# Sixty-four zero bytes per partition, written to the output early, in a kernel that combines two expert outputs

## The chip, the cores and the metric

The kernel runs on one core of a Trainium2 chip. Its time is the device time in microseconds (us) of that core, as a median over several runs. The profile shows one execution of the same program; its span, from the first to the last recorded event, is a little shorter than the time measured.

## The reference: what is computed

For each of 16 x 1024 tokens there are two expert outputs of 512 floats and two weights. The result is their weighted sum.

```python
batch, seq, hidden, n_experts, k = 16, 1024, 512, 8, 2
expert_outputs   # (batch, seq, k, hidden), float32: 67.1 MB
combine_weights  # (batch, seq, k), float32: 0.13 MB

weights = combine_weights[..., np.newaxis]
return np.sum(expert_outputs * weights, axis=2)   # (batch, seq, hidden): 33.6 MB
```

All in all 100.8 MB cross between HBM and SBUF, with three floating-point operations for each element of the result.

## The kernel before

The 16384 tokens are laid over the 128 partitions: 120 tokens a partition in the main part and 8 in a last part. The main part goes through SBUF in ten tiles of 12 tokens a partition (6 MB each), and the last part is an eleventh tile of 4 MB. Four tile buffers rotate, so the fifth load can only start when the first tile's store has read its buffer out. The result of a tile is written over the front half of its buffer and stored from there.

```python
    J, LAST = 12, 8
    main = per - LAST                       # per = 128 tokens a partition
    ...
    def rows(x):
        a = x[0 : P * main, :].rearrange("(p t) f -> p t f", p=P)
        b = x[P * main : n, :].rearrange("(p t) f -> p t f", p=P)
        return lambda t, c: a[:, t : t + c, :] if t < main else b[:, t - main : t - main + c, :]

    eo, cw, o = rows(eo), rows(cw), rows(o)
    ...
    ipool = ctx.enter_context(tc.tile_pool(name="in", bufs=4))

    wt = wpool.tile([P, per * k], dt)

    for t, c in ((0, main), (main, LAST)):  # two weight loads, 120 KB and 8 KB
        nc.scalar.dma_start(
            out=wt[:, k * t : k * (t + c)].rearrange("p (t k) -> p t k", k=k), in_=cw(t, c)
        )

    warm = wpool.tile([P, 1], dt)
    nc.scalar.activation(out=warm, in_=nc.const_aps.tensor(1.0, (P, 1), dt), func=copy)

    for g in range(last + 1):
        et = ipool.tile([P, J, k * h], dt)
        ot = et.rearrange("p j f -> p (j f)")[:, 0 : J * h].rearrange("p (j f) -> p j f", f=h)
        t0, c = g * J, J if g < last else LAST

        # the first tile comes in two pieces: 2 tokens, then 10
        for a, m in ((0, 2), (2, c - 2)) if g == 0 else ((0, c),):
            nc.sync.dma_start(
                out=et[:, a : a + m],
                in_=eo(t0 + a, m),
                max_dma_last_dim=k * h * 4 if g + a == 0 else None,
            )
        if g < last - 1:                    # nine tiles: two VectorE operations and a store
            ...
            nc.vector.tensor_tensor(out=ek, in0=ek, in1=wb, op=mult)                            # L78
            nc.vector.tensor_tensor(out=ot, in0=et[:, :, 0:h], in1=et[:, :, h : 2 * h], op=add) # L79
            nc.scalar.dma_start(out=o(t0, c), in_=ot)                                           # L80
            continue
        ...                                 # the last two tiles share the work with ScalarE
        nc.sync.dma_start(out=o(t0, c), in_=ot[:, 0:c])
```

Loads are issued from SyncE's queue (q1 in the profile). The weights and the stores of the first nine tiles are issued from ScalarE's queue (q10), and the stores of the last two tiles from SyncE's.

The very first load piece is cut into packets of 4096 B (`max_dma_last_dim`); a packet of the other loads is a whole row of 40960 or 49152 B, and of a full tile's store 24576 B.

Of the kernel before, what the change touches and what calls it, by code (L numbers as in the profile page):

```python
# [1 line left out]

# [4 lines left out]


@with_exitstack
def kernel(  # L10
    ctx: ExitStack,
    tc: tile.TileContext,
    expert_outputs: bass.AP,
    combine_weights: bass.AP,
    out: bass.AP,
):

    nc = tc.nc  # L20
    b, s, k, h = expert_outputs.shape
    assert k == 2
    n = b * s
    P = nc.NUM_PARTITIONS
    per = n // P
    assert per * P == n
    J, LAST = 12, 8
    main = per - LAST
    assert main % J == 0
    eo = expert_outputs.rearrange("b s k h -> (b s) (k h)")  # L30
    cw = combine_weights.rearrange("b s k -> (b s) k")
    o = out.rearrange("b s h -> (b s) h")
# [9 lines that stand above are left out]
    dt = mybir.dt.float32  # L42
    mult = mybir.AluOpType.mult
    add = mybir.AluOpType.add
    copy = mybir.ActivationFunctionType.Copy

    last = main // J

    wpool = ctx.enter_context(tc.tile_pool(name="w", bufs=1))
    ipool = ctx.enter_context(tc.tile_pool(name="in", bufs=4))  # L50

    wt = wpool.tile([P, per * k], dt)

    for t, c in ((0, main), (main, LAST)):
        nc.scalar.dma_start(
# [18 lines that stand above are left out]
        if g < last - 1:  # L74

            wb = wt[:, g * J * k : (g + 1) * J * k].unsqueeze(2).to_broadcast([P, J * k, h])
            ek = et.rearrange("p j (k h) -> p (j k) h", k=k)
# [6 lines that stand above are left out]
        for i in range(c):  # L84
            t = t0 + i
            nc.scalar.activation(  # L86
                out=et[:, i, 0:h], in_=et[:, i, 0:h], func=copy, scale=wt[:, 2 * t : 2 * t + 1]
            )
            if g == last:
                nc.vector.scalar_tensor_tensor(  # L90
                    out=ot[:, i, :],
                    in0=et[:, i, h : 2 * h],
                    scalar=wt[:, 2 * t + 1 : 2 * t + 2],
                    in1=et[:, i, 0:h],
                    op0=mult,
                    op1=add,
                )
        if g < last:
            w1 = wt.rearrange("p (t k) -> p t k", k=k)[:, t0 : t0 + c, 1:2]
            x1 = et[:, :, h : 2 * h]  # L100
            nc.vector.tensor_tensor(out=x1, in0=x1, in1=w1.to_broadcast([P, c, h]), op=mult)  # L101
            nc.vector.tensor_tensor(out=ot, in0=et[:, :, 0:h], in1=x1, op=add)  # L102
        nc.sync.dma_start(out=o(t0, c), in_=ot[:, 0:c])


# [1 line left out]
_INS = ['expert_outputs', 'combine_weights']  # L107
_OUTS = [((16, 1024, 512), 'float32')]


# [23 lines left out]
```

## Time and profile before

| what | value |
|---|---|
| time, median of 3 runs | 239.03 us (238.98 to 239.05) |
| span of the profiled execution | 237.3 us |
| VectorE (DVE): L78, 9 times | 116.6 us, 12955 ns each |
| VectorE: L79, 9 times | 59.0 us, 6558 ns each |
| ScalarE (ACT): L86, 20 times | 12.5 us, 707 ns each |
| a tile load of 6 MB, issue to landing | 29.9 us (median of 9) |
| a tile store of 3 MB, issue to landing | 32.7 us (median of 9 from ScalarE's queue) |
| weights, 120 KB and 8 KB, issue to landing | 4.4 and 17.1 us |

In the profile's lists an instruction is named by its source line (L78 is line 78 of the kernel before), its engine, and what it writes and reads. A busy share is the part of the span in which an engine worked. "Issue to landing" runs from the instruction that starts a transfer to the arrival of its last byte, so it holds the time in which the transfer stood in line behind others. The chain of waits is followed back from the last instruction, at each step to what released it.

### The profile page before, as it was taken

To read this page: it belongs to the slowest core of one execution; us is meant where nothing else is said; L and a number is where in the kernel's file an instruction comes from. 1 tells how busy PE (TensorE), PEld (TensorE's weight loads), DVE (VectorE), ACT (ScalarE), POOL (GpSimd) and SP (SyncE) were. 2 spreads that over 40 slices of the span, in tenths; PEclk is the share of its full clock that TensorE was granted. 3 is DMA by queue.
4 is the path that set the end of the run, shared out by engine and by line. 5 is a ranking of instruction groups with operands and counts; after the bars stand their busy time and mean duration, and the time that the engine had idled before them with its cause. 6 is when DMAs were issued, how large, how long until landed. Compare 5 with 4: busy or idle time off the path is not lost.

```text
span 237.3 us, 154 instructions
## 1 busy us (share of the span) xinstructions
DVE 193.9 (82%) x28; ACT 14.0 (6%) x22; POOL 0.2 (0%) x4
## 2 busy tenths in 40 slices
DVE  0008999999999999999999879969996998785710
ACT  2000000000000000000000000000000000740800
POOL 0000000000000000000000000000000000000000
DMA  8999999989899999999897999999997979999997
GB/s 308 443 456 406 398 431 497 398 356 505 356 439 435 427 464 464 398 398 522 348 522 344 452 427 435 464 464 398 398 522 340 530 336 460 458 403 442 402 438 309
DMA packets 3728, 100.80 MB, mean 425 GB/s; under 512 B 528, under 2 KB 656, under 8 KB 912
## 3 DMA queue, kind: packets, MB, share of 16 engines
q1 hardware_dynamic: 2144, 72.35, 71.1%
q10 hardware_dynamic: 1584, 28.44, 27.9%
HBM read 67.24 MB, written 33.55 MB: 425 GB/s over the span
## 4 chain that ended last, share of the span: by engine, by line
DMA 59%; DVE 33%; ACT 2%; DVEq 0%; ACTq 0%; issue 0%; SPq 0%
DMA et<-in_expert_outputs_dram 30%; DMA out_dram<-et 29%; DVE et L78 22%; DVE et L79 11%; ACT et L86 2%; DVE et L90 1%; DVEq L129 0%; ACTq L129 0%; SPq L69 0%; DVEq L78 0%; ACTq L86 0%
## 5 line engine op out<-in xcount | busy, mean ns | idle before, releaser
L78 DVE TENSOR_TENSOR et<-et,wt 128x12288 f32<-128x12288 f32 x9 | 116.6, 12955 | 25.2 <-DMA et<-in_expert_outputs_dram 25.2
L79 DVE TENSOR_TENSOR et<-et 128x6144 f32<-128x6144 f32 x9 | 59.0, 6558 | 0.3
L86 ACT ACTIVATE et<-et,wt 128x512 f32<-128x512 f32 x20 | 12.5, 707 | 209.2 <-DMA et<-in_expert_outputs_dram 209.2
L90 DVE SCALAR_TENSOR_TENSOR et<-et,wt 128x512 f32<-128x512 f32 x8 | 5.6, 748 | 3.9 <-ACT et L86 3.7
L101 DVE TENSOR_TENSOR et<-et,wt 128x6144 f32<-128x6144 f32 x1 | 6.6, 6559 | 2.3 <-DMA et<-in_expert_outputs_dram 2.3
L102 DVE TENSOR_TENSOR et<-et 128x6144 f32<-128x6144 f32 x1 | 6.6, 6559 | 0.9 <-ACT et L86 0.9
L60 ACT ACT_TABLE_LOAD x1 | 1.3, 1283 | 1.7 <-issue 1.7
L60 ACT ACTIVATE warm<-const-float32-1.0 128x1 f32<-128x1 f32 x1 | 0.2, 202 | 0.0
L118 POOL MEMSET const-bfloat16-1.0<- 128x1 bf16 x1 | 0.1, 102 | 0.0
L118 POOL MEMSET const-uint8-127<- 128x1 uint8 x1 | 0.1, 102 | 0.0
L118 POOL MEMSET const-float32-0.0<- 128x1 f32 x1 | 0.1, 99 | 0.2 <-issue 0.2
L118 POOL MEMSET const-float32-1.0<- 128x1 f32 x1 | 0.1, 99 | 0.0
## 6 DMA issues: line engine op xcount, KB each, us to landing
et<-in_expert_outputs_dram SPq DMA_DIRECT2D x9, 6144.0 KB, 29.9
out_dram<-et ACTq DMA_DIRECT2D x9, 3072.0 KB, 32.7
et<-in_expert_outputs_dram SPq DMA_DIRECT2D x1, 5120.0 KB, 17.3
et<-in_expert_outputs_dram SPq DMA_DIRECT2D x1, 4096.0 KB, 25.1
out_dram<-et SPq DMA_DIRECT2D x1, 3072.0 KB, 14.6
out_dram<-et SPq DMA_DIRECT2D x1, 2048.0 KB, 10.0
et<-in_expert_outputs_dram SPq DMA_DIRECT2D x1, 1024.0 KB, 5.4
wt<-in_combine_weights_dram ACTq DMA_DIRECT2D x1, 120.0 KB, 4.4
```

The costliest lines, as they stand in the source:

```text
L60: nc.scalar.activation(out=warm, in_=nc.const_aps.tensor(1.0, (P, 1), dt), func=copy)
L78: nc.vector.tensor_tensor(out=ek, in0=ek, in1=wb, op=mult)
L79: nc.vector.tensor_tensor(out=ot, in0=et[:, :, 0:h], in1=et[:, :, h : 2 * h], op=add)
L86: nc.scalar.activation(out=et[:, i, 0:h], in_=et[:, i, 0:h], func=copy, scale=wt[:, 2 * t : 2 * t + 1])
L90: nc.vector.scalar_tensor_tensor(out=ot[:, i, :], in0=et[:, i, h : 2 * h], scalar=wt[:, 2 * t + 1 : 2 * t + 2], in1=et[:, i, 0:h], op0=mul ...
L101: nc.vector.tensor_tensor(out=x1, in0=x1, in1=w1.to_broadcast([P, c, h]), op=mult)
L102: nc.vector.tensor_tensor(out=ot, in0=et[:, :, 0:h], in1=x1, op=add)
L118: nc = _bacc.Bacc("TRN2", target_bir_lowering=False, num_devices=1)
```

## The change

A small tile of 16 floats a partition is set to zero and written to the output: to the first 64 bytes of the first token's row on each of the 128 partitions. These are rows that the first tile's store later writes in full, so the zeros are overwritten and the result is the same. The first store waits until the zeros have landed. In the built program ScalarE's queue issues the first weight load, then the zeros, then the second weight load; the zeros wait for VectorE's memset.

What it is for: in this kernel the first write to the output in HBM comes with the first tile's store. With the change a tiny write to the same 128 rows comes ahead of it, while the first tile is still being loaded, so that whatever is particular to a first write is met early and with little data.

```diff
     wt = wpool.tile([P, per * k], dt)
 
+
+    zt = wpool.tile([P, 16], dt)
+    nc.vector.memset(zt, 0.0)
+    nc.scalar.dma_start(out=o(0, 1)[:, 0, 0:16], in_=zt)
 
     for t, c in ((0, main), (main, LAST)):
         nc.scalar.dma_start(
```

## The prediction, written before the result was known

> **What bounds the kernel now.** I read the page's summary parts first: busy time by engine, the span in 40 slices, the DMA queues.
>
> ```profile
> DVE 193.9 (82%) x28; ACT 14.0 (6%) x22; POOL 0.2 (0%) x4
> ...
> DMA  8999999989899999999897999999997979999997
> ...
> q1 hardware_dynamic: 2144, 72.35, 71.1%
> q10 hardware_dynamic: 1584, 28.44, 27.9%
> HBM read 67.24 MB, written 33.55 MB: 425 GB/s over the span
> ```
>
> VectorE is busy for 82% of the span, but the two DMA queues together (q1 is SyncE's, q10 ScalarE's) fill 71.1 + 27.9 = 99% of the time of the 16 DMA engines. The trace's records of single packets say it more sharply. A load packet of 49152 B takes 1815 ns and a store packet of 24576 B takes 912 ns, so one DMA engine moves 27 B/ns whichever way it goes, and 16 of them 433 GB/s. All packet times summed and divided by 16 give 234.8 us; the first packet starts at 2.9 us and the last ends at 237.3 us, a stretch of 234.4 us. From the first packet to the last no DMA engine rests. The time is therefore 2.9 us of start, plus the sum of packet times for one engine, plus what lies outside the span (239.03 measured less 237.3, or 1.7 us). Only a change in that sum, or a hole between packets, can move the end.
>
> The chain of waits agrees, and shows which links are passengers (columns: start, length, what):
>
> ```profile
> 1.22 17.29 DMA et<-in_expert_outputs_dram
> ...
> 18.64 12.97 DVE et L78
> ...
> 77.14 30.48 DMA out_dram<-et
> ...
> 107.68 29.89 DMA et<-in_expert_outputs_dram
> ```
>
> VectorE starts at 18.64 us because the first tile's 6 MB have then landed. Later a 3 MB store takes 30 us and the load behind it another 30 us, since both stand in full queues. VectorE has room: after its first start it waits for loads only 25.2 - 18.6 = 6.6 us at L78 (the costliest groups) and 2.3 us at L101.
>
> Two places fall short of the full rate. The first is the start: the 256 packets of 4096 B take 159 ns in most cases but 201 ns on average, 10.6 us too much in all, which is 0.66 us for each of 16 engines; 9.3 of the 10.6 us belong to packets that start before 4.3 us. The second is where the first store comes in. The table by stage shows it as a dip (last column GB/s, before it the DMA share):
>
> ```profile
> 20.00:36.00 16.00, 15.96 (x2) 0.00 (x0) 0.00 (x0) 1.00 1.01 439
> 36.00:52.00 16.00, 15.97 (x3) 0.00 (x0) 0.00 (x0) 1.00 0.95 396
> 52.00:68.00 16.00, 16.00 (x2) 0.00 (x0) 0.00 (x0) 1.00 0.99 429
> ```
>
> A packet's bytes are counted where it starts, so these rows wobble by some 20 GB/s; the packet records settle the size. Of the 1152 load packets of 49152 B, sixteen that start between 42.0 and 42.6 us take 2.23 to 2.42 us instead of 1.815. They are the last ones ahead of the first store's first packets, one on each engine. They carry 8.2 us of excess, and the size as a whole 9.7 us: 9.7 / 16 = 0.60 us for each engine. The store's own packets take 912 ns from the first one on, and none of the ten later stores shows such a stall. So the first write to the output costs the whole machine about 0.6 us, once. That is the only thing in the profile on which this change can act.
>
> **What the skill says.** In "DMA: Bandwidth & Descriptors", section "Back-pressure in remote DMA": stalled writes stall the source engine's other queues too. It speaks of transfers between cores; the trace has a stall of the same shape, load packets of q1 held up at the moment a write of q10 begins. Section "Queues, rings and completion order" of the same page: a DMA engine goes round-robin over its queues, packet by packet. The trace agrees: behind the first weights every 64 B packet of the second weights alternates with one 40960 B packet of a load, which is why 8 KB need 17.1 us to land. Section "Specifications" sets 512 B as the least transfer for line rate, with a read-modify-write below it. The 64 B packets of before take 11 ns each, but they write to SBUF; no run yet shows a 64 B write to HBM. No page that I found speaks of a cost of the first write to a tensor.
>
> **The change part by part.**
> 1. One memset of 128x16 on VectorE. VectorE has nothing to do until 18.64 us. The memsets of before take about 0.1 us (on GpSimd, one element). On the path: 0.
> 2. One more DMA issue on ScalarE's queue. In the built program it stands between the two weight loads and waits for the memset. The two issues of before take 0.97 us together, so 0.5 us more. It delays the second weights, the table load and the warm activation; the first real work on ScalarE starts at 203 us. On the path: 0.
> 3. The packets: 128 of 64 B and 16 of 4 B for the semaphore, so 8 + 1 for each engine. At the 11 and 9 ns of such packets in before that is 0.10 us; should a small write to HBM cost like a 960 B packet (44 ns), 0.36 us. They are added to the sum, since no engine has a hole. I take +0.12 us.
> 4. Waiting on order. The second weights' packets come behind the zeros in the same queue. The zeros will take the eight rounds against 40960 B packets, so they land near 18 us, and the weights go eight rounds against 49152 B packets, 8 x 1.82 = 15 us later, near 33 us. They are first waited for at about 77 us (by the third store, through a shared semaphore) and used at 220 us. The first store waits for the zeros, and is issued at 38.2 us. On the path: 0.
> 5. Semaphores. There are eight for the DMAs in turn, so one DMA more shifts all later ones by a place. I went through every pair in the built program. The one new wait that is not implied by another is that the fourth tile's load waits for the first weights (landed near 5.1 us, load formerly issued near 3 us). Two tiles are still queued ahead then, 30 us of work. On the path: 0.
> 6. The stall. Each row of the output that the first store starts at is touched early. If the first touch is what costs, the 0.60 us at 42 us goes. It need not vanish: it may appear at the zeros' own time instead. The zeros can be issued from about 1.3 us, and packets follow an issue by 2.2 us (0.73 to 2.9 in before), so they may be prepared from 3.5 us on, inside the stretch up to 4.3 us in which the load packets already stall for their own start. What of the 0.60 lies beside that is free; what comes later is paid again. I choose half: -0.30 us.
>
> Sum: 239.03 + 0.12 - 0.30 = 238.85; I say 238.8.
>
> **Rivals.**
> A. The stall only moves. For it: the zeros follow 960 B packets that end only at 5.7 us, by which time the loads run at full rate, and the engines take packets in order. Then 239.03 + 0.12 = 239.15, and VectorE starts near 19.2 instead of 18.64.
> B. The stall has nothing to do with the first touch, but with the first large write or the first turn from loads to stores. For it: it sits in load packets, not in the store's. Then the zeros change nothing at 42 us: again 239.1 to 239.4.
> C. The stall goes and is wholly hidden in the start: 239.03 - 0.60 + 0.12 = 238.55. For it: small packets hold little data back, and the start is a stretch of waiting.
> D. The 128 small writes are slow themselves, each a first touch of its own that holds the engine: 8 stalls of 0.5 us would be 4 us, or 243. Against it: the first store touches eight rows on each engine too, and after its first packets nothing stalls. I give it 2%.
>
> **Range and chances.** A and B together get about as much weight as C and the halfway case. 238.8 lies between; the ends are C with some luck (238.3) and A with dearer small packets (239.5). Three runs of before lie within 0.07 us, so the noise is below these terms. Two per cent is 4.8 us, eight times the only stall there is to save; faster by that is as good as excluded, slower by that needs D.
>
> **What would show it.** Step 6 right: no load packet over 2 us near 42 us, and the row 36:52 at the level of its neighbours. Whether it is saved or moved: VectorE's first start, 18.6 to 18.8 if saved, 19.1 to 19.3 if moved (A). B: the sixteen long packets are still there. Step 3: the zeros' packets, 64 B in q10, at 11 ns or more. Step 4: the landing of the second weights, later by some 15 us, with nobody waiting. The prediction would be wrong if a new wait of SyncE's queue appeared ahead of the fourth or fifth load, or if the sum of packet times moved by over 0.7 us.

## The result, and the profile after

The changed kernel took 240.07 us (median of 5, 239.81 to 240.29) against 239.0 us before (median of 5, 238.98 to 239.05). The ratio is 1.0045, with an interval of 1.0033 to 1.0057: about half a per cent slower. The prediction was 238.8 us, with a range of 238.3 to 239.5, so it was outside.

These are the lines of the page of the changed kernel that answer to those shown of the kernel before.

```profile
DVE 194.0 (81%) x29; ACT 13.9 (6%) x22; POOL 0.2 (0%) x4
...
DMA  8999999999999989999999999899999999999995
GB/s 307 440 462 396 396 495 420 387 462 396 396 433 425 503 363 453 404 519 396 462 396 412 453 404 511 359 433 449 474 396 462 396 453 412 438 416 438 445 414 231
...
q1 hardware_dynamic: 2144, 72.35, 70.6%
q10 hardware_dynamic: 1728, 28.45, 27.8%
HBM read 67.24 MB, written 33.56 MB: 423 GB/s over the span
```

The work is the same: VectorE's busy time has grown by 0.1 us, and 0.01 MB more is written. What differs is the end. In the last of the 40 slices the DMA engines are half busy and move 231 GB/s; before it was 7 tenths and 309 GB/s. The chain of waits of the changed kernel shows that the start is not where the time was lost (columns: start, length, what):

```profile
1.22 16.91 DMA et<-in_expert_outputs_dram
...
18.27 12.97 DVE et L82
...
76.77 30.73 DMA out_dram<-et
...
107.56 32.06 DMA et<-in_expert_outputs_dram
```

VectorE even begins 0.37 us earlier than before (18.27 against 18.64), and up to 107.5 us the chain is level or ahead. The dip at the first store is still there. In the table by stage of the changed kernel (last column GB/s) it is deeper than before, 387 against 396:

```profile
20.00:36.00 16.00, 15.97 (x2) 0.00 (x0) 0.00 (x0) 1.00 1.02 443
36.00:52.00 16.00, 15.96 (x3) 0.00 (x0) 0.00 (x0) 1.00 0.94 387
52.00:68.00 16.00, 16.00 (x2) 0.00 (x0) 0.00 (x0) 1.00 1.00 433
```

And the tail of the changed kernel, microsecond by microsecond (the last two columns are the share of the 16 DMA engines and GB/s of packets that start in the stretch):

```profile
235.00:236.00 1.00, 0.00 (x0) 0.00 (x0) 0.00 (x0) 1.00 0.62 262
236.00:237.00 1.00, 0.00 (x0) 0.00 (x0) 0.00 (x0) 1.00 0.15 66
```

After 236 us only some 0.15 of 16 engines, that is two, still start packets. In the kernel before the same view has no packet that starts after 236 us:

```profile
236.00:237.00 1.00, 0.00 (x0) 0.00 (x0) 0.00 (x0) 1.00 0.00 0
```

The packet records say it exactly. Of the 16 DMA engines of the changed kernel, fourteen write their last completion between 235.8 and 236.1 us, just as in the kernel before (235.7 to 236.2), and two at 237.3. The transfer has landed only when its last engine is done. (The Trainium skill says so in "DMA: Bandwidth & Descriptors", section "Why a DMA increments its semaphore by 16 and not by 1": only the full count of 16 means that all data landed. The trace agrees.)

Two remarks on the packet records. They do not name the DMA engine. The engines' sequences are put together from the records: on one engine a packet starts within some 10 ns of the end of the one ahead of it. And the prediction counted packet times from the trace's zero, which lies 1.1 us ahead of the span's; its packet times are 1.1 us too late (the first packet starts at 1.8 us and the last ends at 236.2). From here on all are counted from the span's start.

Here are two engines of the changed kernel from those sequences, with L for a load packet of 48 KB (1.815 us), S for a store packet of 24 KB (0.912 us), and the excess over these times where there is any:

```
fourteen engines like this:  39.45 L        41.26 L +0.12  43.20 S  44.11 L +0.20  46.11 S  47.02 L  48.83 S
two engines like this:       39.55 L        41.37 S        42.27 L +1.10  45.19 S  46.09 L  47.91 S  48.82 L +0.66
```

The two have taken the first store's packet one turn earlier than the others. They are held for 1.10 and again for 0.66 us, 1.76 us in all, where the fourteen others lose 0.6 on average. Everything after that is in lockstep, so they end over a microsecond behind.

### The profile page after: what moved, and what is told of

The parts are those of the page before. It is cut to its first block, busy times and chain, and to the rows that moved or that the text cites. A ratio compares the mean times of both kernels' runs of the same rounds, so it can differ in the third digit from the quotient of the medians.

```text
span 238.5 us, 157 instructions
## 1 busy us (share of the span) xinstructions
DVE 194.0 (81%) x29; ACT 13.9 (6%) x22; POOL 0.2 (0%) x4
## 4 chain that ended last, share of the span: by engine, by line
DMA 60%; DVE 33%; ACT 2%; DVEq 0%; ACTq 0%; issue 0%; SPq 0%
DMA et<-in_expert_outputs_dram 32%; DMA out_dram<-et 28%; DVE et L82 22%; DVE et L83 11%; ACT et L90 2%; DVE et L94 1%; DVEq L133 0%; ACTq L133 0%; SPq L73 0%; DVEq L82 0%; ACTq L90 0%
```

## The experiments

Theories. **Phase**: the first store reaches the 16 DMA engines while each is in the middle of a 1.8 us load packet, and an engine can take a store packet only when its load packet has ended (its next turn); if the store arrives so that some engines take it a turn apart from the others, those fall behind by about 1 us, and the end follows them. The change only shifts the moment. **Packets**: the zeros' extra small packets cost it. **Same rows**: writing where the first store will write costs it. **First write** (the prediction's): the stall at the first store belongs to the first write to the output.

Already in the first runs the executions of one and the same kernel fell into two groups, about 239.05 and about 240.2 us, with little between them. All executions of the kernel before that were taken beside the experiments come to 216: 144 of them at 238.94 to 239.38 (median 239.05) and 72 at 239.82 to 240.95 (median 240.2). The five of the first comparison were all in the lower group. With a share of one third, chance alone does that once in eight times. It made the change look dearer than it is on average: the 27 executions of the change have a mean of 240.06 us and the 216 of the kernel before one of 239.47, a difference of 0.6 us where the first comparison has 1.07. So what is compared below is above all the share of executions over 239.4 us, the "upper group"; each run of a kernel has between 7 and 22 executions. The ratio beside each time is the one on record for that run against the kernel before; it is not the quotient of two medians, and the shares say more.

**The first store 0.5 us later, with the zeros.**

```diff
+    scratch = wpool.tile([P, 320], dt)
...
+            if g == 0:
+                flat = et.rearrange("p j f -> p (j f)")[:, 0:320]
+                nc.vector.tensor_tensor(out=scratch, in0=flat, in1=flat, op=add)
             nc.vector.tensor_tensor(out=ot, in0=et[:, :, 0:h], in1=et[:, :, h : 2 * h], op=add)
```

> The changed kernel, zeros kept, with one VectorE operation of about 0.4 us put between the first tile's two operations, so that the first store is issued 0.4 us later, at 38.2 us as in the kernel before. Phase theory (the zeros harm only because the first store is issued 0.4 us earlier and its packets then reach two of the 16 DMA engines one turn ahead of the others): all engines take the first store in the same turn again, the last one ends with the others, 239.0 +- 0.3. Packet theory (the extra small packets in ScalarE's queue are what costs) and same-rows theory (writing zeros where the first store writes is what costs): 240.1, as with the change.

Measured: 239.18 us, 2 of 20 executions in the upper group (239.47 and 240.79), ratio 0.9987 (0.997 to 1.0003). The operation delayed the store by 0.53 us. More work on VectorE gave back nearly the whole loss (to within 0.1 us of the kernel before's lower group) while every zero was still written. This is against the packet and the same-rows theory.

**The first store 1.5 us later, without zeros** (the same edit on the kernel before, with 1280 elements).

> The kernel before, no zeros, with one VectorE operation of about 1.4 us between the first tile's two operations. A load packet takes 1.82 us, so the first store then meets the engines' turns where it meets them in the changed kernel (0.4 us earlier is the same as 1.4 later). Phase theory: some engines take it one turn ahead and fall behind, 239.7 to 240.5 without any zeros. Packet and same-rows theories: 239.0 to 239.2, since VectorE is not what bounds.

Measured: 239.84 us, 12 of 12 over 239.4 (239.48 to 240.09); ratio 1.0016 (0.9998 to 1.0034). The table by stage of this run shows a dip as deep as that of the change, with no zeros in the program:

```profile
36.00:52.00 16.00, 16.00 (x2) 0.00 (x0) 0.00 (x0) 1.00 0.97 386
```

In its packet records eleven engines take the first store at 43.2 to 43.5 us and five at 46.0 to 46.1. The time is the one that the phase theory expected, the pattern is not: not a few engines fall behind, but the loss is 1.3 us on average over all 16, and they end late together (236.4 to 236.9 us).

**The zeros to other rows.**

```diff
-    nc.scalar.dma_start(out=o(0, 1)[:, 0, 0:16], in_=zt)
+    nc.scalar.dma_start(out=o(main, 1)[:, 0, 0:16], in_=zt)
```

> The changed kernel with the zeros written to the first rows of the last tile's output instead of the first tile's; the same packets at the same time, but no row shared with the first store. Same-rows theory: 239.0. Phase and packet theories: about 240.1.

Measured: 240.11 us, 8 of 12 in the upper group (239.14 to 240.59), ratio 1.0016 (0.9994 to 1.0037). The shared rows are not needed for the harm.

**A small load in place of the zeros.**

```diff
-    nc.vector.memset(zt, 0.0)
-    nc.scalar.dma_start(out=o(0, 1)[:, 0, 0:16], in_=zt)
+        if t == 0:          # between the two weight loads
+            nc.scalar.dma_start(out=zt, in_=eo(0, 1)[:, 0, 0:16])
```

> The changed kernel without memset and zeros; in their place between the weights a 64 byte load per partition from the first input rows, so 128 packets of the same size in the same queue and no early write. Same-rows theory, and any theory in which the early write matters: 239.0. Packet theory: 240.1. Phase theory: 240.1 if the first store is again issued near 37.8 us, 239.0 if near 38.2.

Measured: 239.49 us, 6 of 12 in the upper group (239.07 to 240.72), ratio 1.0011 (0.999 to 1.0033). A half of 12 executions is not clear of the third of the kernel before, so this run alone does not settle whether the harm needs a write; the run with late weights and no zeros, below, does.

**The change over more executions.**

> The changed kernel as it is, over many more executions. The executions of the kernel before fell into two groups in the first experiments, near 239.05 and near 239.9 to 240.9. Phase theory: the change has the same two groups, near 239.1 to 239.2 and near 240, with a far larger share in the upper one (over half, against 13 of 47). Packet theory: all near 240, none at 239.1 to 239.2.

Measured: 240.08 us, 12 of 14 in the upper group, the other two at 239.09 and 239.16; ratio 1.0009 (0.999 to 1.0027), beside a kernel before that was itself in the upper group in 18 of 46. So the change has both groups, and its lower one is about that of the kernel before.

**The first store 0.5 us later, without zeros** (the edit of the first experiment on the kernel before).

> The kernel before, no zeros, with one VectorE operation of about 0.4 us between the first tile's two operations, so that the first store is issued at about 38.6 us. Phase theory: further from the boundary between two turns, so the upper group empties: 239.05 in nearly all executions. If the two groups had another cause (disturbance from outside), the share of the upper group stays near 13 of 47. Taken from the changed kernel with the same delay (239.18), it gives the price of the zeros alone: about 0.1.

Measured: 239.13 us, 6 of 22 in the upper group (239.51 to 239.99), ratio 0.9982 (0.9969 to 0.9995). The upper group did not empty: this expectation missed. Its upper executions lie lower than those of the kernel before. The profiled one was in the lower group, so what they are is not shown; that they have overshot the other edge is what the table further down suggests.

**4096 zero bytes a partition instead of 64.**

```diff
-    zt = wpool.tile([P, 16], dt)
+    zt = wpool.tile([P, 2 * h], dt)
-    nc.scalar.dma_start(out=o(0, 1)[:, 0, 0:16], in_=zt)
+    nc.scalar.dma_start(out=o(0, 2), in_=zt.rearrange("p (j f) -> p j f", f=h))
```

> The changed kernel with 4096 zero bytes per partition (two whole rows of output) instead of 64; 0.5 MB more to move, 1.2 us. First-write theory (the stall at the first store belongs to the first write of some size, and 64 bytes were too little): the long load packets near 42 us vanish or appear at the zeros, 239.6 or 240.2. Turn theory (the stall belongs to the step from loads alone to loads and stores in turn, whenever a long run of stores begins): it stays at the first store, 240.2 or more.

Measured: 241.09 us (7 executions, 240.99 to 241.23), ratio 1.0058 (1.0037 to 1.0079). The 4 KB packets went to HBM from 17.4 us on at 159 ns each, with no stall. (In this built program the zeros are issued behind both weight loads, so the second weights are not late.) The stall at the first store, 0.59 us for each engine, stayed where it was. One engine took the store a turn late, lost 1.49 us and ended at 238.1, the others at 237.0 to 237.3. So the first-write theory falls.

**Real output early, no zeros.** The first tile's two leading tokens are multiplied, added and stored on their own.

```diff
-            wb = wt[:, g * J * k : (g + 1) * J * k] ...
+            for a, m in ((0, 2), (2, c - 2)) if g == 0 else ((0, c),):
+                ...     # multiply, add and store tokens a .. a + m
+                nc.scalar.dma_start(out=o(t0 + a, m), in_=ot[:, a : a + m])
```

> The kernel before, no zeros; the first tile's two leading tokens a partition, which land first, are multiplied, added and stored on their own at about 8 us (4096 bytes a partition of real output, no byte more in all), and the other ten follow. First-write theory: the stall goes to about 10 us or vanishes, 238.5 to 239.0. Turn theory: a stall of about 0.6 us for each engine stays at the second store near 40 us: 239.0, or 239.8 where the engines take it in two turns.

Measured: 239.56 us (12 executions, 239.42 to 239.96), ratio 1.0001 (0.9985 to 1.0018). The early store (4096 bytes a partition, issued at 9.6 us, its packets from 17.4 us on) brought no stall. The stall moved with the first large store, which now comes 3 us earlier: load packets that start from 37 us on take up to 1.6 us too long, and two engines take that store a turn late. Again it is not the first write.

**Zeros kept, the second weights moved away.**

```diff
-    for t, c in ((0, main), (main, LAST)):
+    def weights(t, c):
...
+    weights(0, main)
...
+            if g == 1:      # the copy makes the load wait for the tile; issued at 57.6 us, behind the second store
+                nc.scalar.activation(out=wt[:, k * main : k * main + 1], in_=ot[:, 0, 0:1], func=copy)
+                weights(main, LAST)
```

> The changed kernel, zeros kept in their place, but the second weights are loaded only after the second tile's store (near 58 us). So no 64 byte packet is left between the landing of the first tile (18 us) and the first store. Late-weights theory (the zeros push the second weights' packets behind the first tile, where they delay each engine's turns by about 0.1 us against the first store, and the last engine slips into an earlier turn): the share of executions in the upper group falls from 17 of 19 to about that of the kernel before (31 of 98), the lower group at 239.05 to 239.15. Zeros theory (what counts is the early write or the packets of the zeros themselves, before 18 us): 17 of 19 stays.

Measured: 239.65 us, ratio 1.0024 (1.0009 to 1.0039), 22 executions: 16 at 239.19 to 239.79 and 6 at 240.07 or above, one of them 242.29. The lower group is itself 0.4 us higher, because of a side effect. The small load now stands in ScalarE's queue between two stores; in the profile the store packets cease from 84 to 101 us, and a second stall, 0.2 to 0.5 us for each engine, lies between 117 and 130 us. If one takes the 6 as the upper group, the share is that of the kernel before; by the line at 239.4 us it would be 20 of 22. The two are not cleanly apart, so I count this run as inconclusive.

**No zeros, the second weights late.**

```diff
...     # weights(t, c) is the load of one part, as above
+    weights(0, main)
+    scratch = wpool.tile([P, 1024], dt)
+    nc.vector.memset(scratch, 1.0)
...
+    for _ in range(12):
+        nc.scalar.activation(out=scratch, in_=scratch, func=copy)
+    nc.scalar.activation(out=wt[:, k * main : k * main + 1], in_=scratch[:, 0:1], func=copy)
+    weights(main, LAST)
```

> The kernel before, no zeros at all, with the second weights' load held back by ScalarE (twelve copies of a scratch tile) to about 18 us, so that its 128 packets of 64 bytes run between the landing of the first tile and the first store, as in the changed kernel. Late-weights theory: the upper group takes over half of the executions, 239.8 to 240.7, with no zeros. Zeros theory: as the kernel before, about a third in the upper group.

Measured: 240.16 us, 14 of 22 in the upper group (to 240.8), beside 22 of 75 of the kernel before; ratio 1.0019 (1.0003 to 1.0035). No zeros are left in this program, only small packets between the first tile and the first store. Its page ends as that of the change does:

```profile
DMA  8999999999999979999999999899999997999995
GB/s 306 439 461 396 396 519 399 391 461 395 395 437 420 527 329 461 412 511 395 461 395 395 465 441 478 383 408 461 461 395 461 395 519 342 456 410 426 461 404 220
```

One engine took the first store at 41.3 us, the others at 43.2 to 43.5; it ended at 237.5, they at 235.7 to 236.0.

**A shorter delay of the first store, without zeros** (160 elements).

> The kernel before with one VectorE operation of about 0.2 us between the first tile's two, so that the first store comes 0.2 us later: half way to the kernel that was delayed by 0.4 us and had 6 of 22 in the upper group, and as far from the boundary as the changed kernel with 0.4 us, which had 1 of 20. Phase theory: at most 3 executions in 20 in the upper group, the rest at 239.05; better than the kernel before on average. If the groups do not depend on the moment of the first store: a third in the upper group.

Measured: 239.08 us, 1 of 22 over 239.4 (239.41), ratio 0.9991 (0.9981 to 1.0). The delay came to 0.36 us. The operation that does it, in the chain of waits of this run:

```profile
18.16 12.97 DVE et L79
...
31.16 0.34 DVE scratch L82
...
31.52 6.56 DVE et L83
```

The mean of the 22 is 239.11, of the 75 executions of the kernel before beside it 239.43. It does not lower the best time; it takes the upper group away, and so beats both kernels on average. One and the same round of runs holds both counts, 1 of 22 and 22 of 75.

**Shorter load packets.**

```diff
-                max_dma_last_dim=k * h * 4 if g + a == 0 else None,
+                max_dma_last_dim=k * h * 4 if g + a == 0 else 4 * k * h * 4 if g in (2, 3) else None,
```

> The kernel before with the loads of the third and fourth tile, those on the way when the first store comes, cut into packets of 16 KB instead of 48 KB: a turn lasts 0.6 us instead of 1.8. Phase theory: an engine that is a turn out of step then loses at most about 0.4 us instead of 1.1, so all executions lie at 239.1 to 239.5 and the upper group is gone. If the stall of about 0.6 us for each engine also belongs to the long load packets, it shrinks and the time falls to 238.6 to 238.9. Theories in which the first write costs: 239.1, and a third at 240.

Measured: 240.05 us (20 executions, 239.77 to 242.07), ratio 1.003 (1.0013 to 1.0046). A miss for every theory: the stall grew from 0.6 to 1.1 us for each engine, spread over two to four packets between 39.7 us and the store's first packet. So the stall is not a share of a long load packet. Nor did the variation go.

**The three last runs.** First the change again.

> The changed kernel again, to settle how often it lands in the upper group: 17 of 19 so far, against 28 of 46 in the three kernels that delay the second weights without writing the first store's rows. If late weights are the whole cause, the share here falls towards 28 of 46 (about 13 of 22); if writing the same rows or the first store's wait on the zeros adds something, it stays near 17 of 19 (19 or more of 22).

Measured: 240.35 us, 7 of 8 in the upper group, the other at 239.04; ratio 1.003 (1.0006 to 1.0054). All executions of the change together: 24 of 27 in the upper group. The three kernels that delay the second weights without writing these rows have 28 of 46. So something beyond the late weights seems to be at work, on numbers that are small.

Then the kernel before, with a profile of its own.

> The kernel before once more, with a profile of its own. Phase theory: about a third of the executions near 240; if the profiled one is among them, one or two of the 16 DMA engines take the first store a turn ahead of the others, and the last load packet starts before the store's turn later than 2.7 us after the store's issue; if it is near 239.05, all take it in the same turn and that distance is 2.2 to 2.7 us.

Measured: 239.17 us, 6 of 14 in the upper group, ratio 1.0009 (0.999 to 1.0029). The profiled execution was in the lower group (239.14), and all 16 engines took the first store in one turn, at 43.2 to 43.5 us. No profile was got of an upper execution of the kernel before itself. The distances in its expectation carry the same 1.1 us too much as the packet times; the table below has them right.

Last, the second weights late and the first store 0.36 us later.

> The kernel without zeros and with the second weights late (14 of 22 in the upper group), with the first store delayed by 0.2 us as well. Phase theory: the delay outweighs the 0.1 us that the late packets cost each engine, so nearly all executions lie at 239.15 to 239.3 and at most 4 of 22 in the upper group. If late weights cost by themselves, not through the moment of the first store: over half stay in the upper group.

Measured: 239.18 us, none of 14 in the upper group (239.09 to 239.25), ratio 0.9988 (0.9975 to 1.0002). Without the delay it was 14 of 22, in an earlier round; in the round of this run the kernel before had 19 of 43 and the change 7 of 8. So the late packets act through the moment of the first store; what they cost by themselves is 0.1 us (239.18 against 239.08).

**The profiles side by side.** The three kernels in which the transfers themselves differ (4096 zero bytes, the early store, the shorter packets) are left out. For each, the gap from the end of the last packet of the first tile to VectorE's start; the distance d from the first store's issue to the latest start of a load packet among the 16 engines in the turn about it; and the engines that took the store in another turn than the rest.

| profile | gap, us | d, us | out of turn | span, us |
|---|---|---|---|---|
| kernel before | 0.73 | 1.46 | none | 237.3 |
| kernel before, again | 0.73 | 1.49 | none | 237.4 |
| zeros elsewhere | 0.75 | 1.52 | none | 237.4 |
| load for zeros | 0.73 | 1.57 | none | 237.3 |
| before, store 0.36 later | 0.59 | 1.28 | none | 237.3 |
| late weights, store 0.36 later | 0.53 | 1.34 | none | 237.2 |
| before, store 0.53 later | 0.70 | 0.98 | none | 237.2 |
| zeros, second weights moved | 0.53 | 1.67 | none | 237.6 |
| change, first profile | 0.54 | 1.70 | 2 early | 238.5 |
| change, second | 0.57 | 1.67 | 2 early | 238.4 |
| change, third | 0.59 | 1.68 | 1 early | 238.7 |
| late weights, no zeros | 0.58 | 1.71 | 1 early | 238.7 |
| change, store 0.53 later | 0.52 | 1.15 | 1 late | 237.7 |
| before, store 1.53 later | 0.58 | 0.12 | 5 late | 238.1 |

In these profiles an edge lies at about 1.67 us: beyond it an engine takes the store early. The other edge is not as sharp: with d = 0.98 none is late, with 1.15 one is. There the 16 engines lie further apart, 0.68 us from the earliest to the latest against 0.42; that this is the reason is not shown.

## Why the prediction was wrong, point by point

**What bounds the kernel: right, but read too coarsely.** It is the DMA engines, as said. But the prediction summed the packet times, divided by 16 and concluded that "only a change in that sum, or a hole between packets, can move the end". Sum divided by 16 is the mean engine. The sum hardly moved (234.8 us before, 234.9 after), yet the end moved by a microsecond, because two engines were held up longer than the others (1.76 us against 0.6). This is the step that failed. The time of this kernel is that of its slowest DMA engine, and no line of the page before shows how the engines differ; the last slice of the page after does. The prediction's own account of 239.03 us does not close either: 2.9 us of start, 234.8 of packets and 1.7 outside the span make 239.4. The recorded packet times overlap a little (234.8 us of them in a stretch of 234.4), and of the 2.9 us only 1.8 lie ahead of the first packet; the other 1.1 lie behind the last one.

**Steps 1 to 3, memset, issue and packets: right.** The memset took 72 ns on an idle engine, and the issue 0.44 us. The 64 B packets to HBM took 11 ns each, as those to SBUF do. A read-modify-write, of which the Trainium skill speaks for under 512 B ("DMA: Bandwidth & Descriptors", section "Specifications"), is not visible in the engines' time. The lower group of the change lies at 239.04 to 239.16 (three executions), of the kernel before at 239.05, so the price of the zeros alone is 0 to 0.1 us; +0.12 was predicted.

**Step 4, "on the path: 0": wrong.** The landings are as predicted. The issue list of the changed kernel (KB each, us to landing) has the zeros near 18 us and the second weights near 32:

```profile
wt<-in_combine_weights_dram ACTq DMA_DIRECT2D x1, 120.0 KB, 3.3
out_dram<-zt ACTq DMA_DIRECT2D x1, 8.0 KB, 16.6
wt<-in_combine_weights_dram ACTq DMA_DIRECT2D x1, 8.0 KB, 30.8
```

Nobody waits for them, but they are not free. 65 to 116 of their 128 packets now run between the landing of the first tile and the first store (none in the kernel before), and at 11 ns each delay an engine's turns there by 0.04 to 0.08 us on average. The runs without zeros and with late weights (14 of 22, and none of 14 once the store is delayed) show that late packets are enough to raise the share. But 0.04 to 0.08 us does not by itself bridge the 0.2 us between the kernel before's d and the edge: the profiles with late packets and a long gap stand at 1.52 and 1.57, with no engine out of turn. What bridges the rest is taken up below.

**Step 5, semaphores: right.** The new wait, the fourth load for the first weights, is there, and lasts 1.0 us of queue time with nothing behind it. The view of SyncE's waits in the changed kernel:

```profile
SPq L73 <- DMA out_dram<-et: 174.0, 7, 45.8
...
SPq L73 <- DMA wt<-in_combine_weights_dram: 1.0, 1, 1.0
```

**Step 6, the stall: wrong.** The term of -0.30 us did not come: without it the prediction would have been 239.15, which is the change's lower group. The stall neither vanished nor moved to the zeros: at the first store the engines lose 0.71 us on average with the change, 0.59 without. Rival B, that the stall has nothing to do with the first touch, was the right one of the four on this point, and its 239.1 to 239.4 is nearly the lower group of the change; what it lacked was the upper. The reading of the start in step 6 was off as well, since packets follow an issue by 1.1 us (0.73 to 1.8), not 2.2. The sign to look for, VectorE's first start, came out at 18.27, earlier than any rival said, and had nothing to do with the zeros' stall: it lies anywhere from 18.05 to 18.64 in the profiles of all kernels.

**Rivals C and D** fell: nothing was gained, and no small write held an engine for 0.5 us.

**The range** was built from sums of small terms and from three runs within 0.07 us. It had no term for a second group of executions, which the kernel before has too, in a third of its executions. Small noise in three runs was taken for small noise.

**What is shown and what is open.** Shown: that engines out of turn at the first large store carry the loss (four profiles over 238.3 us of span with one or two early engines, against none in the profiles of the lower groups); that a delay of the first store of 0.36 us all but removes the upper group (1 of 22 and none of 14), with no change in the transfers; and that late small packets enlarge it without zeros. Open: why the change's share (24 of 27) is above that of late weights alone (28 of 46). The table offers a candidate only: the gap between landing and VectorE's start takes two values, 0.52 to 0.59 and 0.70 to 0.75, and in all five profiles with 64 zero bytes to the first store's rows it was the short one, which adds about 0.17 us to d. But the rows alone do not set it: with 4096 zero bytes to the same rows it was 0.76 us, and it was short in four of the table's profiles without zeros. What sets it is not known. The kernel before has an upper group of its own; as no upper execution of it has a profile, that it comes of the same thing is argued, not shown. Nor is it shown why a delay of 0.53 us without zeros left 6 of 22 above 239.4 us where 0.36 us left one. Open too: what the stall of 0.6 us itself is. It comes with the first store of 20 KB or more a partition, not with earlier writes of 64 or 4096 bytes, and it does not shrink with shorter load packets.

## What to carry to other kernels

Where transfers fill the whole time, ask for the slowest of the 16 DMA engines, not for their mean: the last slice of the page, or a table of the last microseconds, shows whether they end together. Where a store joins a stream of long load packets, look whether it reaches all engines in the same turn; in this kernel a few tenths of a microsecond in its issue, made with a small operation on an engine that has room, decided over 1 us at the end. And before a change of half a per cent is judged, take twenty executions and look for groups: three or five can all fall into one.

## What the runs showed of the hardware that was not expected

A DMA engine alternates between the two queues packet by packet, as the Trainium skill says in "DMA: Bandwidth & Descriptors", section "Queues, rings and completion order"; the traces agree, with load and store packets in turn (a transfer's 4 byte completion packet, 9 ns, takes a turn of its own). Not expected was what it costs to be early at the start of that alternation: in the four profiles the early engines ended 1.1 to 1.7 us behind the mean of the others, never made up in the 190 us that follow. Nor was it expected that a 64 byte write to HBM takes an engine 11 ns and a 4 KB write 159 ns, the same as loads of those sizes, while the first large store stalls all 16 engines for 0.6 us.
